# Keys and values of the second block by Strassen's product, and scores issued one head ahead

## Chip, cores and metric

The kernel runs on one core of a Trainium2 chip. The metric is the device time of one execution in microseconds; the kernel before takes 1948.06 us, the median of 3 runs (1947.14 to 1948.31).

## The reference

Two transformer-like blocks in float32 on 256 tokens of width 2048. The first (an mLSTM and a gated delta net side by side) is not touched. The second takes its output x and a context ctx of 256 tokens:

```python
hx = rmsnorm(h, norm_g) * (1.0 + scale) + shift            # 256 x 2048
hc = rmsnorm(ctx, norm_g) * (1.0 + scale_c) + shift_c      # 256 x 2048
qa, ka, va, ga, qb, kb, vb, gb = jnp.split(hx @ wi, 8, axis=-1)     # 1024 columns each
ka_c, va_c = jnp.split(hc @ wi[:, DA_WIDTH:3 * DA_WIDTH], 2, axis=-1)
kb_c, vb_c = jnp.split(hc @ wi[:, NA_OFF + NA_WIDTH:NA_OFF + 3 * NA_WIDTH], 2, axis=-1)
oa = diff_attention(qa, ka, va, ka_c, va_c, ...) * jax.nn.silu(ga)      # 8 heads, 2 softmaxes each, rope
ob = neighbourhood_attention(qb, kb, vb, kb_c, vb_c, ...) * jax.nn.silu(gb)   # 8 heads, bias
h = h + gate * (jnp.concatenate([oa, ob], axis=-1) @ w_out)
```

Only keys and values are needed for both inputs: the same weights meet hx and hc, 512 rows together. Queries and gates are needed for hx alone.

## The kernel before

Every product of activations and weights is made of three matmuls in float32r: an operand is split into hi (a copy, ACT) and lo (the rest, DVE), and hi hi, hi lo and lo hi are summed in PSUM. `split_w` (L127) splits a weight tile of 128x1024 that `load_w` fetched on SP's queue (4 raw buffers, 3 pairs of split ones); the two split instructions have a higher priority. `proj_T` (L136) has the weights stationary and 256 tokens moving and gives a transposed result (queries, keys); `proj` (L152) has tokens stationary and 512 weight columns moving (values, gates, outputs). With both inputs given, one split feeds twice the matmuls. The large PSUM tiles of both come from a pool of two (`psA`, two banks each); `side` gives single banks from a pool of four.

Block 2 (L923 on) goes through `kv`, `queries`, `gate2` and `diff_attn` for each of two groups of four heads of attention a, then through `kv` for both groups of b, and then `queries` and `near_attn` (with its gate) for each. `kv` computes keys and values and leaves them in SBUF (kT as hi and lo, V). In attention a the keys pass `rope` (L954) and their lo parts go through "nb" buffers (two of them) to the other half of the partitions by DMA on POOL's queue. The heads' work is short matmuls between instructions of DVE and ACT: two scores, maximum, exp, combination, four transposes (`pv`, L1019), product with V. `rep` (L935) is a table for attention b that is written to DRAM early on POOL's queue.

The order on each engine is made by a planner ahead of time: a list with priorities in program order, against simulated times of the instructions and the release of buffers. Later matmuls can so be put between those of a head; on the chip each engine then runs its list in order. Pools "big" tags Ah and Al hold hch and hcl (split hc), Bh and Bl hold hxh and hxl.

## Time and profile before

| | |
|---|---|
| median of 3 runs | 1948.06 us |
| the profiled execution | 1945.1 us |
| its span, first to last instruction | 1943.1 us |
| PE matmul busy | 1923.5 us, 12118 matmuls |
| DVE busy | 1336.9 us |
| ACT busy | 874.1 us |
| mean granted clock of TensorE | 0.997 |

A row of the page names line, engine, operation and tiles (out<-in), its count, and after the bar the busy time and the mean duration in ns; then the idle time of the engine before it, and what ended that. Matmul durations are modelled and overlap, so two matmuls that follow each other are priced by the distance of their starts.

### The profile page before, as it was taken

What the parts mean: (1) busy time and instruction counts of PE and PEld (TensorE: products, weight loads), DVE (VectorE), ACT (ScalarE), POOL (GpSimd) and SP (SyncE); (2) the same over time, 40 slices, a digit from 0 to 9 for tenths busy, and PEclk for the clock granted to TensorE, in tenths of its full rate; (3) what the DMA queues carried; (4) which work ended last, traced back from release to release, by engine and by line L of the source; (5) the groups of instructions that cost most, each with busy time, mean ns of one, the idle gap of its engine ahead of it and who ended that gap; (6) DMA issues with size and microseconds to landing.
All of it is one profiled execution on the core that took longest, in us unless ns stands there. A gap on an engine that the chain in (4) does not pass through costs nothing.

```text
span 1943.1 us, 30816 instructions
## 1 busy us (share of the span) xinstructions
PE 1923.5 (99%) x12118; PEld 1686.6 (87%) x12118; DVE 1336.9 (69%) x1956; ACT 874.1 (45%) x1179; POOL 240.0 (12%) x347
## 2 busy tenths in 40 slices
PE   9999999999999999999999999999999999999998
PEld 9989898999878898888888888888989989889876
DVE  6978686784648999758998856646554642269755
ACT  7645444453334443444444544634434432235553
POOL 1011010111101222002121000211111100002211
PEclk9999999999999999999999999999999999999999
DMA  9555454453546788658888767556234422279844
GB/s 293 172 167 168 142 180 151 143 178 131 168 154 211 237 262 266 204 181 298 283 281 290 252 209 240 167 137 206 94 93 157 125 76 90 96 262 329 266 148 165
DMA packets 118817, 372.70 MB, mean 192 GB/s; under 512 B 14904, under 2 KB 21480, under 8 KB 118672
## 3 DMA queue, kind: packets, MB, share of 16 engines
q1 hardware_dynamic: 95296, 314.44, 48.4%
q0 software_dynamic: 16864, 45.57, 8.4%
q10 hardware_dynamic: 6512, 10.72, 1.9%
q8 instruction: 95, 1.56, 0.3%
q14 instruction: 50, 0.41, 0.1%
HBM read 359.89 MB, written 7.64 MB: 189 GB/s over the span
## 4 chain that ended last, share of the span: by engine, by line
PE 92%; DVE 2%; DMA 2%; issue 2%; ACT 1%; POOL 0%; POOLq 0%; ACTq 0%; DVEq 0%
PE pN L163 17%; PE pN L162 17%; PE pN L164 17%; PE pT L147 10%; PE pT L149 10%; PE pT L148 10%; DMA kT<-klo 1%; DVE lo L131 1%; PE tp L1028 1%; PE p L595 1%; PE tp L1023 1%; DMA w<-in_out_dram 1%; PE pT L247 1%; ACT hi L130 0%; PE wp L642 0%
## 5 line engine op out<-in xcount | busy, mean ns | idle before, releaser
L131 DVE TENSOR_TENSOR lo<-w,hi 128x1024 fp32r<-128x1024 f32 (+1 forms) x555 | 672.9, 1215 | 423.2 <-ACT hi L130 411.5
L130 ACT ACTIVATE hi<-w 128x1024 fp32r<-128x1024 f32 (+1 forms) x555 | 580.5, 1048 | 824.7 <-PE pN L164 465.5
L163 PE MATMUL pN<-lo,uh 128*128 128x512 f32 x768 | 306.2, 399 | 0.0
L162 PE MATMUL pN<-hi,uh 128*128 128x512 f32 x768 | 305.0, 397 | 0.0
L164 PE MATMUL pN<-hi,ul 128*128 128x512 f32 x768 | 304.4, 396 | 0.0
L147 PE MATMUL pT<-uh,hi 128*128 128x256 f32 x896 | 255.5, 285 | 2.2 <-ACT kq L744 1.9
L149 PE MATMUL pT<-uh,lo 128*128 128x256 f32 x896 | 256.5, 286 | 0.0
L148 PE MATMUL pT<-ul,hi 128*128 128x256 f32 x896 | 255.7, 285 | 0.0
L162 PEld LDWEIGHTS pN<-hi,uh 128*128 128x128 f32 x768 | 144.8, 189 | 34.1
L163 PEld LDWEIGHTS pN<-lo,uh 128*128 128x128 f32 x768 | 144.8, 189 | 33.7 <-DVE lo L131 0.3
L164 PEld LDWEIGHTS pN<-hi,ul 128*128 128x128 f32 x768 | 144.8, 189 | 33.5
L147 PEld LDWEIGHTS pT<-uh,hi 128*128 128x128 f32 x896 | 168.7, 188 | 5.2 <-ACT kq L744 2.1
L149 PEld LDWEIGHTS pT<-uh,lo 128*128 128x128 f32 x896 | 168.8, 188 | 2.9 <-issue 2.4
L148 PEld LDWEIGHTS pT<-ul,hi 128*128 128x128 f32 x896 | 168.8, 188 | 1.8 <-issue 1.2
L464 DVE SCALAR_TENSOR_TENSOR ma<-m,sc,ma 128x512 f32<-128x512 f32 x240 | 169.6, 745 | 0.0
L149 PE MATMUL pT<-hxh,lo 128*128 128x256 f32 x512 | 144.8, 283 | 0.0
L147 PE MATMUL pT<-hxh,hi 128*128 128x256 f32 x512 | 144.8, 283 | 0.0
L148 PE MATMUL pT<-hxl,hi 128*128 128x256 f32 x512 | 144.6, 282 | 0.0
L162 PE MATMUL pN<-hi,hxh 128*128 128x512 f32 x256 | 101.5, 397 | 1.1 <-ACT hi L130 1.1
L163 PE MATMUL pN<-lo,hxh 128*128 128x512 f32 x256 | 101.4, 396 | 1.3 <-DVE lo L131 1.3
L454 POOL DMA_DIRECT2D m<-in_w_mod_dram x128 | 69.7, 545 | 263.2 <-DVE ma L464 208.9
L164 PE MATMUL pN<-hi,hxl 128*128 128x512 f32 x256 | 101.1, 395 | 0.0
(620 smaller groups left out, 3380.6 us busy)
## 6 DMA issues: line engine op xcount, KB each, us to landing
w<-in_dn_qkv_dram SPq DMA_DIRECT2D x88, 512.0 KB, 3.3
m<-in_w_mod_dram POOLq DMA_DIRECT2D x128, 256.0 KB, 4.1
w<-in_dn_z_dram SPq DMA_DIRECT2D x32, 512.0 KB, 3.3
w<-in_ml_v_dram SPq DMA_DIRECT2D x32, 512.0 KB, 3.6
w<-in_ml_z_dram SPq DMA_DIRECT2D x32, 512.0 KB, 4.2
w<-in_ml_o_dram SPq DMA_DIRECT2D x32, 512.0 KB, 4.1
w<-in_gate_a_dram SPq DMA_DIRECT2D x32, 512.0 KB, 4.4
w<-in_gate_b_dram SPq DMA_DIRECT2D x32, 512.0 KB, 4.4
```

Of the source, the lines that this page charges most:

```text
L130: act.activation(hi, raw, AF.Copy)
L131: ve.tensor_tensor(lo, raw, hi.bitcast(F32), ALU.subtract)
L147: pe.matmul(o, hi[:, k, :], xh[:, kt, :], start=(kt == 0), stop=False)
L148: pe.matmul(o, hi[:, k, :], xl[:, kt, :], start=False, stop=False)
L149: pe.matmul(o, lo[:, k, :], xh[:, kt, :], start=False, stop=(kt == KT - 1))
L162: pe.matmul(ps[:, t, :], xh[:, kt, s], hi[:, k, :], start=(kt == 0), stop=False)
L163: pe.matmul(ps[:, t, :], xh[:, kt, s], lo[:, k, :], start=False, stop=False)
L164: pe.matmul(ps[:, t, :], xl[:, kt, s], hi[:, k, :], start=False, stop=(kt == KT - 1))
L247: pe.matmul(o, hl[wt][:, k, :], x[:, 4 * c + k, :], start=(c == 0 and a == 0 and k == 0), stop=(c == 3 and a == 2 and k == 3))
L454: (gp if g < 8 else nc.sync).dma_start(raw, d["w_mod"][g, kt])
L464: ve.scalar_tensor_tensor(a, raw, s, a, ALU.mult, ALU.add)
L595: pe.matmul(p0, kq[:, h, 0, 0:P], kq[:, h, :, :], start=True, stop=True)
```

## The change

Each pair of key tiles, and each 512 columns of values, becomes a 2x2 block product (rows: tokens of x and of ctx; inner: halves of 2048; columns: two tiles or two halves). Seven products replace eight, in the form with 15 sums: four sums of token blocks (S1 to S4, made and split once), four of weight blocks (T1 to T4, for each pair or quarter, split after), seven of results. To make the token sums, hx and hc are kept unsplit too: hf and hcf become four tiles each, `mod_T` writes the full hx into hf, and the context part and out_b's part move to a second pool, opened after out_a. All keys and values (but group 0 of va, which stays plain and comes first) are computed before the attention and stored in DRAM (kd, vd); `kv` loads them back. The keys of a land in kraw, in the place of hch; er, eight buffers for exp, takes the same place after it. In both attentions the scores of the next head are issued before the transposes of this one; gate 0 of b comes before the heads.

The diff, cut to its core:

```diff
-        hf = hfp.tile([P, 2, 4, 512], F32, name="hf")
+        hf = [hfp.tile([P, 2, 512], F32, tag="hf", name="hf", bufs=4) for _ in range(4)]
+        tb = hfp.tile([P, 2, 4, 512], F32, tag="tb", name="tb")
...
+        sA.close()
+        hcp = sR.enter_context(tc.tile_pool(name="hcp", bufs=1, side="right", reuse_waits="tile"))
+        hcf = [hcp.tile([P, 4, T], F32, tag="hcf", name="hcf", bufs=4) for _ in range(4)]
+        s1h = hcp.tile([P, 8, T], F32R, name="s1h")
...
-            for n in range(4):
-                ct = o1.tile([P, 4, T], F32, tag="xr", name="ct")
...
-                    act.activation(hch[:, k, :], c_, AF.Identity, bias=sh)
-                    ve.scalar_tensor_tensor(hcl[:, k, :], c_, sh, hch[:, k, :].bitcast(F32), ALU.add, ALU.subtract)
...
+                act.dma_start(hcf[n], d["ctx_t"][n * 512:(n + 1) * 512, :].rearrange("(k p) t -> p k t", p=P))
...
+                    act.activation(c_, c_, AF.Identity, bias=modT[:, 2, k:k + 1])
+                act.activation(hch[:, k4, :], hcf[n], AF.Copy)
+                ve.tensor_tensor(hcl[:, k4, :], hcf[n], hch[:, k4, :].bitcast(F32), ALU.subtract)
...
+            for c in range(2):
+                s1 = hcf[2 + c]
+                ve.tensor_tensor(s1, hcf[c], s1, ALU.add)
+                act.activation(s1h[:, 4 * c:4 * c + 4, :], s1, AF.Copy)
...
+        kd = {ab: tc.dram_tile([8, P, 2, T], F32, name="kd" + ab) for ab in "ab"}
...
+        with ExitStack() as s5:
...
+            s2h, s4h = (st.tile([P, 8, T], F32R, name=nm) for nm in ("s2h", "s4h"))
...
+            def value0(i):
+                vp = proj(d["va"], 0, [(HX, HC)[i]])[0]
+                o = st.tile([P, 2, 512], F32, tag="stg", name="stg", bufs=4)
+                act.activation(o, vp, AF.Copy)
+                gp.dma_start(vd["a"][0][:, 2 * i:2 * i + 2, :], o)
...
+            value0(1)
+            value0(0)
+            v4 = lambda a: a.rearrange("p (a b) t -> p a (b t)", a=2)
+            lo1, lo2, lo4 = [], [], []
+            for c in range(2):
+                h1, h2, f1, f2 = hf[c], hf[2 + c], v4(hcf[c]), v4(hcf[2 + c])
+                ve.tensor_tensor(f1, h1, f1, ALU.subtract)
+                ve.tensor_tensor(h1, f2, h1, ALU.subtract)
+                ve.tensor_tensor(h2, h2, h1, ALU.subtract)
+            for full, hi, lo, pool in ((hcf[0:2], hch, hcl, None), (hcf[2:4], s1h, lo1, hcp),
+                                       (hf[0:2], s2h, lo2, hcp), (hf[2:4], s4h, lo4, hfp)):
+                for c in range(2):
+                    f = full[c] if full[c].shape[1] == 2 else v4(full[c])
+                    k4 = slice(4 * c, 4 * c + 4)
+                    h_ = v4(hi[:, k4, :])
+                    if hi is not s1h:
+                        act.activation(h_, f, AF.Copy)
+                    if pool is not None:
+                        tg = "hcf" if pool is hcp else "hf"
+                        lo.append(pool.tile([P, 4, T], F32R, tag=tg, name="sl", bufs=4))
+                    l_ = v4(lo[:, k4, :] if pool is None else lo[c])
+                    ve.tensor_tensor(l_, f, h_.bitcast(F32), ALU.subtract)
...
+            A11, A12, A22 = (of(hxh), of(hxl)), (of(hxh, 8), of(hxl, 8)), (of(hch, 8), of(hcl, 8))
+            S1, S2 = (of(s1h), of2(lo1)), (of(s2h), of2(lo2))
+            S3, S4 = (of(hch), of(hcl)), (of(s4h), of2(lo4))
+            TT = hfp.tile([P, 4, 1024], F32, tag="tb", name="TT")
+            ALL = slice(0, T)
...
+            def keys(ab, j):
...
+                B11, B12, B21, B22 = (raw_w(w[j + c, r], 8, P) for r in range(2) for c in range(2))
+                T1, T2, T3, T4 = (TT[:, i, :].rearrange("p (k c) -> p k c", k=8) for i in range(4))
+                ps = [psA.tile([P, 2, 2, T], F32, tag="p", name="pK").rearrange("p a b t -> p (a b) t"),
+                      side([P, 2, T], name="pK"), side([P, 2, T], name="pK")]
+                P1, P6, P5, P3, P7, P4, P2 = (p[:, i] for p, n in zip(ps, (4, 2, 1)) for i in range(n))
...
+                def prod(ps, A, B):
+                    hi, lo = split_w(B, 8, P)
+                    for k in range(8):
+                        pe.matmul(ps, hi[:, k, :], A[0](k, ALL), start=(k == 0), stop=False)
+                        pe.matmul(ps, hi[:, k, :], A[1](k, ALL), start=False, stop=False)
+                        pe.matmul(ps, lo[:, k, :], A[0](k, ALL), start=False, stop=(k == 7))
+                prod(P1, A11, B11)
+                act.activation(c1, P1, AF.Copy)
+                prod(P2, A12, B21)
+                ve.tensor_tensor(o[:, 0, 0], P2, c1, ALU.add)
+                ve.tensor_tensor(T1, B12, B11, ALU.subtract)
+                ve.tensor_tensor(T3, B22, B12, ALU.subtract)
+                ve.tensor_tensor(T2, B22, T1, ALU.subtract)
+                ve.tensor_tensor(T4, B21, T2, ALU.subtract)
+                prod(P3, S4, B22)
+                prod(P5, S1, T1)
+                prod(P6, S2, T2)
+                ve.tensor_tensor(c1, P6, c1, ALU.add)
+                ve.tensor_tensor(u4, P5, c1, ALU.add)
+                ve.tensor_tensor(o[:, 1, 0], P3, u4, ALU.add)
+                prod(P7, S3, T3)
+                ve.tensor_tensor(c1, P7, c1, ALU.add)
+                ve.tensor_tensor(o[:, 1, 1], P5, c1, ALU.add)
+                prod(P4, A22, T4)
+                ve.tensor_tensor(o[:, 0, 1], P4, c1, ALU.add)
+                for c in range(2):
+                    gp.dma_start(kd[ab][j + c], o[:, c])
...
+            def values(ab, g):
...
+                w = d["v" + ab]
+                pp = [psA.tile([P, 2, 512], F32, tag="p", name="pV") for _ in range(2)]
+                P1, P2, P3, P4 = (pp[i][:, b, :].rearrange("p (t c) -> p t c", t=2) for i in range(2) for b in range(2))
+                P5, P6, P7 = (side([P, 2, T], name="pV") for _ in range(3))
...
+                    for t in range(2):
+                        s = slice(t * P, (t + 1) * P)
+                        for k in range(2):
+                            kt = 2 * q + k
+                            pe.matmul(ps[:, t, :], A[0](kt, s), hl[0][:, k, :], start=(kt == 0 and t == 0), stop=False)
+                            pe.matmul(ps[:, t, :], A[0](kt, s), hl[1][:, k, :], start=False, stop=False)
+                            pe.matmul(ps[:, t, :], A[1](kt, s), hl[0][:, k, :], start=False, stop=(kt == 7 and t == 1))
...
+                H = (slice(0, T), slice(T, 512))
+                for q in range(4):
+                    W1, W2 = raw_w(w[g, q], 2, 512), raw_w(w[g, q + 4], 2, 512)
+                    B11, B12, B21, B22 = W1[:, :, H[0]], W1[:, :, H[1]], W2[:, :, H[0]], W2[:, :, H[1]]
+                    TQ = TT[:, 2 * (q % 2):2 * (q % 2) + 2, :].rearrange("p a (b k c) -> p a b k c", b=2, k=2)
+                    hi, lo = (wsp.tile([P, 2, T], F32R, tag=tg, name=tg) for tg in ("hi", "lo"))
+                    with tc.high_priority(offset=100):
+                        act.activation(hi, B11, AF.Copy)
+                        ve.tensor_tensor(lo, B11, hi.bitcast(F32), ALU.subtract)
+                    prod(P1, A11, (hi, lo), q)
+                    hl = split_w(W2, 2, 512)
+                    prod(P2, A12, [x[:, :, H[0]] for x in hl], q)
+                    prod(P3, S4, [x[:, :, H[1]] for x in hl], q)
+                    ve.tensor_tensor(TQ[:, 0, 0], B12, B11, ALU.subtract)
+                    ve.tensor_tensor(TQ[:, 0, 1], B22, B12, ALU.subtract)
+                    ve.tensor_tensor(TQ[:, 1, 1], B22, TQ[:, 0, 0], ALU.subtract)
+                    ve.tensor_tensor(TQ[:, 1, 0], B21, TQ[:, 1, 1], ALU.subtract)
+                    for a, pr in enumerate((((P5, S1), (P7, S3)), ((P4, A22), (P6, S2)))):
+                        hl = split_w(TQ[:, a].rearrange("p b k c -> p (b k) c"), 4, T)
+                        for b in range(2):
+                            prod(*pr[b], [x[:, 2 * b:2 * b + 2, :] for x in hl], q)
+                c1 = st.tile([P, 2, T], F32, tag="tm", name="tm", bufs=2)
+                act.activation(c1, P1, AF.Copy)
+                def put(r, c, a, b):
+                    o = st.tile([P, 2, T], F32, tag="stg", name="stg", bufs=4)
+                    ve.tensor_tensor(o, a, b, ALU.add)
+                    gp.dma_start(vd[ab][g][:, 2 * r:2 * r + 2, H[c]], o)
+                put(0, 0, P2, c1)
+                ve.tensor_tensor(c1, P6, c1, ALU.add)
+                u4 = st.tile([P, 2, T], F32, tag="tm", name="tm", bufs=2)
+                ve.tensor_tensor(u4, P5, c1, ALU.add)
+                put(0, 1, P3, u4)
+                ve.tensor_tensor(c1, P7, c1, ALU.add)
+                put(1, 1, P5, c1)
+                put(1, 0, P4, c1)
...
+            for ab in "ab":
+                for j in range(0, 8, 2):
+                    keys(ab, j)
+                for g in range(2):
+                    if (ab, g) != ("a", 0):
+                        values(ab, g)
+        sR.close()
...
         def rope(ps, scale):
-            a = a2.tile([P, 2, T], F32, tag="nb", name="ra")
-            act.activation(a, ps, AF.Copy, scale=scale)
+            a = ps
+            if scale is not None:
+                a = a2.tile([P, 2, T], F32, tag="nb", name="ra")
+                act.activation(a, ps, AF.Copy, scale=scale)
...
-                ps = proj_T(d["k" + ab], 4 * g + 2 * j, 2, [HX, HC])
...
-            vps = proj(d["v" + ab], g, [HX] if split_v else [HX, HC])
...
+            if not roped:
+                raw = kT[:, 1].bitcast(F32)
+                gp.dma_start(raw, kd[ab][4 * g:4 * g + 4].rearrange("j p c t -> p j c t"))
+                for j in range(2):
+                    hh = slice(2 * j, 2 * j + 2)
+                    act.activation(kT[:, 0, hh], raw[:, hh], AF.Copy)
+                    ve.tensor_tensor(kT[:, 1, hh], raw[:, hh], kT[:, 0, hh].bitcast(F32), ALU.subtract)
...
+                    for c in (1, 0):
+                        src = kraw[:, 4 * g + 2 * j:4 * g + 2 * j + 2, c, :]
+                        src, lo = (src, a2.tile([P, 2, T], F32, tag="nb", name="klo")) if c else rope(src, None)
+                        lo = lo.bitcast(F32R)
...
+            gp.dma_start(V, vd[ab][g])
...
+                    e = er[:, en[0] % 8, :]
+                    en[0] += 1
+                    act.activation(e, sp, AF.Exp, bias=nm, accum_out=s0[:, h, i:i + 1])
...
+            U_ = [(t, h) for t in range(2) for h in range(4)]
+            nxt = scores(*U_[0])
+            for n, (t, h) in enumerate(U_):
+                e, nxt = nxt, scores(*U_[n + 1]) if n < 7 else None
+                if h == 0:
+                    o_ = side([P, 4, P], name="o_")
+                pv(e, V, h, o_[:, h, :])
+                if n == 3:
+                    G = gate2(g, "a")
...
+            G = gate2(g, "b", O[:, 1].rearrange("p a b c -> p a (b c)")) if g == 0 else None
...
+            U_ = [(h, t) for h in range(4) for t in range(2)]
+            nxt = scores(*U_[0])
+            for n, (h, t) in enumerate(U_):
+                e, nxt = nxt, scores(*U_[n + 1]) if n < 7 else None
+                o_ = pv(e, V, h)
+                act.activation(O[:, t, h, :], o_, AF.Copy, scale=sn[:, t, h:h + 1])
...
+        kraw = big.tile([P, 8, 2, T], F32, tag="Ah", name="kraw")
+        for j in range(0, 8, 2):
+            gp.dma_start(kraw[:, j:j + 2], kd["a"][j:j + 2].rearrange("j p c t -> p j c t"))
+        two = big.tile([P, 2, 2, 4, T], F32R, tag="Al", name="two")
+        QL = [a2.tile([P, 2, 4, T], F32R, tag="O", name="qlo", bufs=1), two[:, 1]]
+        for qlo in QL:
+            for i, r in enumerate(R):
+                gp.memset(qlo[R[1 - i], i].bitcast(F32), 0.0)
+        KA = [kv(0, "a", True)]
+        QA = [queries(0, "a", True, None, QL[0])]
+        KA.append(kv(1, "a", True))
+        er, en = big.tile([P, 8, 512], F32, tag="Ah", name="er"), [0]
+        diff_attn(0, *KA[0], QA[0], QL[0])
+        QA.append(queries(1, "a", True, two[:, 0], QL[1]))
+        diff_attn(1, *KA[1], QA[1], QL[1])
```

## Rows read from the trace of the kernel before

**Rows 1.** The page, table of engines: busy us, share of the span, instructions.
```profile
PE 1923.5 (99%) x12118; PEld 1686.6 (87%) x12118; DVE 1336.9 (69%) x1956; ACT 874.1 (45%) x1179; POOL 240.0 (12%) x347
```

**Rows 2.** Stages: length, PE, PEld, DVE, ACT, POOL busy (instructions), clock, DMA.
```profile
1243.00:1870.00 627.00, 624.55 (x4024) 564.75 (x4023) 345.10 (x474) 254.59 (x365) 76.95 (x90) 1.00 0.50 159
600.00:800.00 200.00, 200.00 (x1072) 171.79 (x1071) 190.38 (x284) 88.52 (x116) 40.48 (x71) 1.00 0.77 250
1236.00:1257.00 21.00, 21.00 (x156) 19.68 (x155) 16.77 (x28) 15.82 (x26) 8.99 (x13) 1.00 0.47 151
1340.00:1470.00 130.00, 130.00 (x803) 116.06 (x802) 74.41 (x115) 53.86 (x85) 17.55 (x18) 1.00 0.37 113
1686.00:1870.00 184.00, 183.93 (x1076) 160.61 (x1075) 129.07 (x172) 84.97 (x125) 24.56 (x30) 1.00 0.75 254
```

**Rows 3.** Timeline of PE, first and last of 99 starts of 256 columns.
```profile
1261.50 0.28 PE L149 MATMUL pT<-hxh,lo 128*128 128x256 f32 x1
...
1273.13 0.28 PE L148 MATMUL pT<-hcl,hi 128*128 128x256 f32 x1
```

**Rows 4.** Timeline of PE, first and last of 47 starts of 512 columns.
```profile
1602.52 0.39 PE L162 MATMUL pN<-hi,hxh 128*128 128x512 f32 x1
...
1613.21 0.40 PE L163 MATMUL pN<-lo,hch 128*128 128x512 f32 x1
```

**Rows 5.** DVE by line and form: busy us, mean ns, idle before.
```profile
L131 DVE TENSOR_TENSOR lo<-w,hi 128x1024 fp32r<-128x1024 f32 x539 | 662.2, 1231 | 414.4 <-ACT hi L130 403.5 <-PE tp L1023 7.8 <-issue 0.3
...
L1050 DVE TENSOR_REDUCE nm<-sp 128x1 f32<-128x512 f32 x32 | 20.9, 683 | 12.0 <-PE sp L1048 11.9
...
L1057 DVE SCALAR_TENSOR_TENSOR e<-e,fl,e 128x512 f32<-128x512 f32 x16 | 12.0, 751 | 0.5
...
L1098 DVE TENSOR_TENSOR sp<-sp,nb 128x256 f32<-128x256 f32 x16 | 6.8, 428 | 8.1 <-PE sp L1097 8.1
...
L960 DVE TENSOR_TENSOR rb<-rb,cfb 128x512 f32<-128x512 f32 x8 | 7.7, 965 | 0.1
...
L1056 DVE SCALAR_TENSOR_TENSOR fl<-fl,nlam,s 128x1 f32<-128x1 f32 x16 | 6.6, 412 | 0.5
...
L959 DVE STREAM_SHUFFLE rb<-ra 128x512 f32<-128x512 f32 x8 | 5.9, 740 | 0.1
...
L987 DVE TENSOR_TENSOR klo<-pT,kT 64x512 fp32r<-64x512 f32 x8 | 5.5, 685 | 1.4 <-ACT kT L986 1.3
...
L1151 DVE TENSOR_TENSOR y<-pN,mr 128x512 f32<-128x512 f32 x6 | 3.8, 681 | 2.1 <-PE pN L164 2.1
```

**Rows 6.** ACT by line and form.
```profile
L130 ACT ACTIVATE hi<-w 128x1024 fp32r<-128x1024 f32 x539 | 570.8, 1060 | 821.0 <-PE pN L164 465.5 <-PE pT L148 250.5 <-issue 73.1
```

**Rows 7.** Chain of waits, whole run: start us, us, what.
```profile
1272.36 13.41 DMA kT<-klo
...
1367.23 0.89 PE o__13119 L1028 x8
```

**Rows 8.** DMA issues: count, KB each, median us to landing.
```profile
hd<-hf POOLq DMA_DIRECT2D x4, 512.0 KB, 5.9
...
kT<-klo POOLq DMA_DIRECT2D x8, 128.0 KB, 4.5
...
rep<-rb POOLq DMA_DIRECT2D x1, 930.0 KB, 21.9
```

**Rows 9.** Timeline of DVE at the first rope; in brackets idle before and releaser.
```profile
1271.37 0.69 DVE L987 TENSOR_TENSOR klo<-pT,kT 64x512 fp32r<-64x512 f32 x1 [0.66 <-ACT kT L986]
...
1285.90 0.01 DVE L959 LOAD_MASK_SELECT rb<-ra  x1 [10.08 <-DMA kT<-klo]
...
1303.92 0.01 DVE L959 LOAD_MASK_SELECT rb<-ra  x1 [2.92 <-DMA kT<-klo]
```

**Rows 10.** Timeline of PE at the same place.
```profile
1291.72 0.50 PE L162 MATMUL pN<-hi,hxh 128*128 128x512 f32 x1 [1.11 <-ACT hi L130]
1292.98 0.50 PE L163 MATMUL pN<-lo,hxh 128*128 128x512 f32 x1 [0.76 <-DVE lo L131]
```

187 lines of the change are left out of this document (92 added, 95 removed).

## The prediction

> **What bounds the kernel now.** I read the page's table of engines first: PE is busy 1923.5 us, 99% of the span, DVE 69% [rows 1]. A busy PE is not a full one, so the second view is the busy time by stage [rows 2]. The change lies in block 2, which runs from 1243 us on; there PE is idle for 2.45 of 627 us, DVE for 45%. The third view is the timeline of PE inside a pure stream: 98 matmuls of 256 columns start in 11.63 us, 0.1187 us each [rows 3]; 46 of 512 columns in 10.69 us, 0.2324 us each [rows 4]. The profile's 0.28 and 0.39 us for one of them overlap the next, so the distance of starts is the price. Block 2 is a queue of matmuls at that pace with next to no holes: a matmul taken away is time saved, a hole put in is time lost.
>
> **What is removed.** Keys: the change works on a pair of head tiles; before, 2 tiles x 2 halves x 8 k x 2 inputs x 3 = 192 matmuls of 256 columns, now 7 products x 8 k x 3 = 168. Eight pairs (four of ka, four of kb) save 192 x 0.1187 = 22.8 us. Values: a 512-column unit was 192 matmuls of 512 columns (44.6 us), is 7 x 4 x 12 = 336 of 256 (39.9 us). Three of four units change (va 0 stays as it was): 14.2 us. Together -37.0 us. The 2.45 us of holes [rows 2] lie where the prologue of the first keys is redone; I count -2.
>
> Here a rule speaks against the change. Two halves cost 0.2374 us where one whole costs 0.2324 [rows 3, 4], so cutting a matmul costs 5 ns, and that is in the sum. The Trainium skill ("TensorE: Matmul & The Clock Gate", Back-to-back issue gap) gives a sustained 131 ns at 512 columns and 81 ns at 128; an estimate from that page for 256, 98 ns, would make the values 23 us dearer and the keys 19 us cheaper, a loss of some 4 us before any wait. This trace disagrees with both figures.
>
> **What is added on DVE and ACT, and what hides it.** A pair of keys needs 7 splits in place of 4: 7 lo subtractions of 1.231 us, 4 weight sums of the same 128x1024 size (as the same row), 7 additions out of PSUM of 0.428 us: 16.5 us of DVE beside 168 x 0.1187 = 19.9 us of PE; ACT 7 x 1.060 = 7.4 us [rows 5, 6]. A value unit: per quarter one half split (0.685), three whole ones (1.231), four sums of 128x512 (0.685), at the end 7 additions of 0.685: 33.3 us of DVE beside 39.9. So DVE stands at 83% in this stage. Cover: from 600 to 800 us DVE is busy 190.4 of 200 us and PE 200 [rows 2]. I take the work itself as hidden.
>
> Waits in the stage, two kinds. (a) The products P7 and P4 of a pair lie in one PSUM bank. No row of before shows a matmul that waits for a read of the other half of its bank; if P4 waits for the addition that reads P7, a pair loses the end of a matmul (0.28 us [rows 3]) and 0.43 of DVE: between 0 and 8 x 0.71 = 5.7 us. I take 2, nearer to nothing, as matmuls of the next pair, in other banks, can stand in between. The Trainium skill ("PSUM — Partial Sum Buffer", PSUM bank collisions raise a hardware error) has PE's write and DVE's read of one bank kept apart by the program; by that rule alone the term is 5.7. (b) Value units hold both large PSUM tiles: P3 of the next unit waits for five or six additions of 0.69 us, 4.1 us, less the 2.85 us of its P1 and P2; three changes of unit, 0 to 1.5 us each: 3.
>
> **The start.** The token sums (S1 to S4) need the finished hx. Between 1236 and 1257, where hx is made, DVE is busy 16.8 of 21 us [rows 2]. Six sums and eight lo subtractions, 14 x 1.23 = 17 us, come after or into that; also the splits of va 0 (one per 2.8 us of PE now, where a key split fed 5.7 us) and the first pair's. From 1236 to P3's start at about 1272 (22.3 us of va 0 from 1243, P1 and P2 5.7, transposes 1) DVE has 36 us, and is asked for the 16.8 of that row, five more splits (6.2), three of the pair (3.7) and 17: 44; P5 behind it needs the weight sums, 4.9 + 1.2 more in 2.85 us. Bounds 0 (all fits idle time) and 8 + 3 = 11; I take 6.
>
> The plain parts of block 1 that move (the ctx statistics to after out_a, four copies of hch, the S1 sums) lie beside 89 us of out_b matmuls; ACT adds 6 x 1.06 us. If that cover failed, the stage would lose these 6 us. New DMAs on POOL's queue: 16 stores of keys and 12 of values of 256 KB, 2 of va 0; 4 + 2 + 4 loads back. Each store lies tens of us ahead of its load.
>
> **Attention a, where the cover goes.** Before, heads of diff_attn ran between K/V matmuls, DVE 74.4 of 130 us [rows 2]. Now queries and gates alone are left. A head costs DVE 2 x 0.683 + 0.751 + 0.412 = 2.53 us (a reciprocal left out), PE 4 x 0.2324 + 8 x 0.111 = 1.82 us [rows 5, 7]. Over the part: PE 45.5 (queries) + 44.6 (gates) + 16 x 1.82 = 119 us; DVE 32 splits (39.4), key and query rope and splits (eight ropes of 0.740 + 0.965 + 0.685, 24 half splits of 0.685: 35.6), heads 40.5, gates 2.4: 118 us. DVE comes level with PE, so what DVE loses is no longer given back.
>
> Two losses. First, the rope of the keys: kraw takes the place of hch, so its loads start when the last product ends (some 5.9 us, as for hd [rows 8]). Then eight pieces pass two "nb" buffers, each freed when its kT DMA lands (4.5 us). Before, DVE stood 10.08 us for such a landing [rows 9], which took 13.41 us [rows 7]; the DMA had been queued on POOL's queue behind rep (930 KB, 21.9 us). PE's holes from it were 1.11 and 0.76 us [rows 10], since three splits held 17 us of key matmuls. Three splits of queries hold 3 x 2.85 = 8.5 us, and "rep" is still ahead of these DMAs: 13.4 - 8.5 = 5 us. What is queued behind the wait on DVE are the query splits, and PE behind them. Second, er takes kraw's place, so no exp runs before the keys of both groups are done: 5.9 + four times 8.3 us (a rope's 2.4, two half splits, a landing) + rep's 21.9 = 61 us at most. PE has queries 0, gate 0, queries 1 until then, 68 us, if the planner puts them ahead; then eight heads run uncovered, 8 x (2.53 - 1.82) = 6 us. If only queries 0 stands ahead, PE waits 61 - 22.8 = 38 us. Bounds 0 and 38; I take 5 + 6 and 2 for the shorter landings (2.92 us of DVE's wait at the next, not all of it PE's) = 13, nearer to what the holes in rows 10 show.
>
> **Attention b and the end.** K/V of b were already done before near_attn; in 1686 to 1870 PE is full, DVE 129 of 184 [rows 2]. Scores one head ahead help the uncovered last heads: -1 (0 to -3).
>
> **Sum**, against the profiled execution (span 1943.1, its time 1945.1 us; the median of the runs is 3.0 above): -37 - 2 + 5 + 6 + 13 - 1 = -16, so 1929 there, 1932 as a median.
>
> **Rivals.** (1) All waits are filled: -37 - 2 - 3 + 4 = -38, 1910. For it: 627 us with 2.45 idle, by the same planner. Against: DVE level with PE in attention a. (2) DVE becomes the bound of the product stage: its additions wait for the end of a product, with splits queued behind. At 0.66 us for each of seven (as DVE waits for ACT in [rows 9]), a pair is 21.1 us of DVE to 19.9 of PE: 8 x 1.2 = 10 us more, 1942. Against: DVE at 95% with a full PE. (3) Slower: PE stands in front of the first heads until the keys of both groups are roped, because matmuls later in its queue can't pass a waiting one. Price up to 38 us; from 29 us there on (with 6 + 5 - 1 elsewhere) the gain of 39 is gone; at 38 it is +9, 1957. For it: the 13.4 us landing that DVE waited for in full. Against: 68 us of other matmuls are at hand. (4) A matmul's fixed part eats the saving: the products are 240 matmuls more and 86,016 columns less (38.2 us at 0.444 ns a column, from the two streams). At 5 ns each the 240 cost 1.2 us; at 159 ns nothing is saved, and with the waits above (24) it is 1972. Against: two streams of this very form at 5 ns [rows 3, 4]. The Trainium skill's figures above would be an estimated 65 ns.
>
> **Chances.** Forecast (1921 to 1943) 0.50, (1) 0.22, (2) 0.10, (3) 0.16, (4) 0.02. About 0.2%, 4 us, is what a measurement of this kernel tells from no change. Faster: 0.47 + 0.22 + 0.05 = 0.74; same: 0.03 + 0.05 + 0.02 = 0.10; slower 0.16. The range runs from (1) to the middle of (3): 1910 to 1953.
>
> **What would show it.** PE's matmuls go from 12118 to 12118 + 240 (2304 of K/V become 2544), DVE's busy time up by about 183 us (8 x 11.6 + 3 x 23.4 + 20). Pairs of keys should start every 20 us, value units every 40. Start: a hole before P3 and P5 of the first pair. Attention a: an idle PE between the end of the products and the first exp, DVE waiting for kT. I am wrong if the products run slower than 0.12 us a matmul, if DVE's share of the stage exceeds 95%, or if the hole in front of the first heads is over 25 us.

## The result, and the profile after

The changed kernel takes **1969.8 us** (median; 1967.8 to 1971.9), the kernel before 1948.2 in the same session: a ratio of **1.0112, 95% interval [1.0095, 1.0130]**. It is 21.6 us slower where 16 us faster was forecast, and outside the range. The profiled execution took 1970.46 us, its span 1968.7, 25.6 us more than before's 1943.1.

The page of the changed kernel, busy us of each engine, its share and its instructions (the answer to [rows 1]):
```profile
PE 1904.7 (97%) x12358; PEld 1683.4 (86%) x12358; DVE 1500.9 (76%) x2161; ACT 926.7 (47%) x1236; POOL 264.4 (13%) x389
```
PE has the 240 matmuls more that were forecast and is busy 18.8 us less, and yet the span is longer. So PE stands idle or runs at a lower clock somewhere. The windows say where (start:end, length, then busy us of PE, its weight loads, DVE, ACT and POOL, granted clock, DMA share, GB/s):
```profile
1130.00:1200.00 70.00, 64.27 (x265) 51.34 (x264) 50.69 (x61) 44.76 (x77) 1.84 (x3) 0.95 0.74 248
1240.00:1280.00 40.00, 36.90 (x164) 29.85 (x164) 37.33 (x48) 28.46 (x40) 6.64 (x9) 0.91 0.47 155
1280.00:1577.00 297.00, 296.83 (x2493) 295.65 (x2492) 230.84 (x273) 119.78 (x128) 22.98 (x36) 1.00 0.42 145
1577.00:1640.00 63.00, 41.86 (x222) 35.77 (x222) 30.62 (x39) 22.39 (x28) 17.69 (x24) 0.84 0.67 178
1640.00:1760.00 120.00, 110.92 (x688) 97.72 (x687) 97.16 (x151) 66.69 (x110) 26.80 (x33) 0.97 0.54 165
1760.00:1850.00 90.00, 88.72 (x561) 78.95 (x560) 80.61 (x130) 50.01 (x84) 19.32 (x24) 1.00 0.79 267
1850.00:1900.00 50.00, 44.39 (x233) 35.10 (x232) 43.18 (x68) 25.33 (x49) 8.39 (x10) 0.97 0.90 305
```
These are out_b, the start of block 2, the product stage, the beginning of attention a, its heads, its end with attention b, and attention b's last heads with the beginning of the output product. Where [rows 2] had 2.45 us idle in 627, the beginning of attention a alone has 21 in 63, and at 0.84 of the clock. For the loss with the clock in it I use one measure throughout, **lost time**: for each matmul the distance to the next start, less the median distance of its width in the same trace, summed over a stretch. Only distances above the median count; the shorter ones, some 10 us in each of the three kernels, are left out. The stretches are fixed times, and a faster kernel is further on in its work at the same time, so sums to the end are safer to compare than single rows.

| lost time, us | before | changed | repaired (below) |
|---|---|---|---|
| 1000 to 1130 (out_a) | 1.3 | 1.0 | 6.3 |
| 1130 to 1200 (out_b) | 0.6 | 9.8 | 2.5 |
| 1240 to 1280 (start) | 1.2 | 6.9 | 5.7 |
| 1280 to 1577 (product stage) | | 3.1 | 4.9 |
| 1577 to 1640 | | 26.1 | 8.9 |
| 1640 to 1760 | | 15.6 | 9.6 |
| 1760 to the end | 7.0 | 18.6 | 10.3 |
| 1200 to the end | 18.5 | 70.6 | 39.7 |

(In the kernel before, products and attentions share the stretch from 1280 to 1760, with 9.9 us lost in all.) From 1130 on the change loses 61.3 us more; the matmuls themselves (the medians, summed from there to the end) need 757.8 us for 794.4, 36.6 less. That makes 24.7 us, where the spans differ by 25.6.

**The product stage is as forecast.** In 1280 to 1577 PE is full and DVE at 78%; the waits of that window list none for PE. The starts keep the pace of [rows 3], 0.12 us:
```profile
1319.74 0.28 PE L1013 MATMUL pK<-hxh,lo 128*128 128x256 f32 x1
1319.86 0.28 PE L1011 MATMUL pK<-hxh,hi 128*128 128x256 f32 x1
1319.98 0.28 PE L1012 MATMUL pK<-hxl,hi 128*128 128x256 f32 x1
1320.10 0.28 PE L1013 MATMUL pK<-hxh,lo 128*128 128x256 f32 x1
```
The Trainium skill's figures for the gap between matmuls ("TensorE: Matmul & The Clock Gate", Back-to-back issue gap), by which the products would have gained nothing, are not what this trace shows. P7 and P4 of a pair never met in their bank: in all eight pairs 1.5 us or more of other matmuls stand between them, as the forecast argued, and DVE's read of P7 is over before P4 begins (in the second pair 1319.82 and 1322.00). So the Trainium skill's rule that the program keeps PE's writes and DVE's reads of one bank apart ("PSUM — Partial Sum Buffer", PSUM bank collisions raise a hardware error) cost no wait here.

**The beginning of attention a.** PE's timeline (start us, us of one, what; in brackets the idle time before and what ended it):
```profile
1605.59 0.40 PE L164 MATMUL pN<-hi,hxl 128*128 128x512 f32 x1
1605.82 0.40 PE L162 MATMUL pN<-hi,hxh 128*128 128x512 f32 x1
1621.91 0.80 PE L163 MATMUL pN<-lo,hxh 128*128 128x512 f32 x1 [15.69 <-DVE lo L131]
1622.50 0.63 PE L164 MATMUL pN<-hi,hxl 128*128 128x512 f32 x1
1622.93 0.63 PE L162 MATMUL pN<-hi,hxh 128*128 128x512 f32 x1
```
A product of the first gate stands 15.69 us for a split, and afterwards matmuls start 0.43 us apart instead of 0.23: the granted clock is at the lower of its two levels (1.2 of 2.4 GHz) after the hole. Why the split was late, DVE's timeline:
```profile
1600.44 1.41 DVE L1163 TENSOR_TENSOR klo<-kraw,kT 64x512 fp32r<-64x512 f32 x2 [5.33 <-DMA kT<-klo]
1601.88 1.23 DVE L131 TENSOR_TENSOR lo<-w,hi 128x1024 fp32r<-128x1024 f32 x1
1620.01 0.01 DVE L1134 LOAD_MASK_SELECT rb<-kraw  x1 [16.90 <-DMA kT<-rb]
1620.65 1.21 DVE L131 TENSOR_TENSOR lo<-w,hi 128x1024 fp32r<-128x1024 f32 x1
```
The split (L131) was queued behind the next key rope (L1134), which waited 16.90 us for a kT piece to free its nb buffer, where [rows 9] had 10.08. POOL's timeline shows what stood ahead of that piece:
```profile
1583.21 1.06 POOL L1166 DMA_DIRECT2D V<-vda  x2
1584.27 0.64 POOL L1165 DMA_DIRECT2D kT<-klo  x1
1586.14 0.66 POOL L1165 DMA_DIRECT2D kT<-klo  x1
1586.79 0.85 POOL L1108 DMA_DIRECT2D rep<-rb  x1
1590.42 1.31 POOL L1165 DMA_DIRECT2D kT<-rb  x2 [2.77 <-DVE rb L1163]
```
The chain of waits has that piece as its longest link there (start, us), and the DMA issues of 1580 to 1640 give the times to landing:
```profile
1591.14 28.73 DMA kT<-rb
```
```profile
V<-vda POOLq DMA_DIRECT2D x2, 1024.0 KB, 10.6
rep<-rb POOLq DMA_DIRECT2D x1, 930.0 KB, 30.7
kT<-klo POOLq DMA_DIRECT2D x4, 128.0 KB, 16.5
```
A piece of 128 KB took 28.7 us, against 13.41 in [rows 7] and 4.5 in [rows 8]; rep took 30.7 for 21.9. The two V loads ahead of it are the change's own.

**Out_b.** DVE there:
```profile
1155.78 5.22 DVE L888 SCALAR_TENSOR_TENSOR hcf<-hcf,gx,rsb 128x256 f32<-128x256 f32 x13
1160.93 0.68 DVE L898 TENSOR_TENSOR hf<-xr,fw 128x512 f32<-128x512 f32 x1
1161.53 1.21 DVE L131 TENSOR_TENSOR lo<-w,hi 128x1024 fp32r<-128x1024 f32 x1
1172.33 1.22 DVE L883 SCALAR_TENSOR_TENSOR xr<-hf,xr 128x1024 f32<-128x1024 f32 x1 [3.25 <-DMA xr<-in_x_dram]
```
Thirteen modulations of ctx stand in a row ahead of a split, later an x tile comes late; PE waits 2.64 us for the first split, 3.09 us at the second place, and the window's clock is 0.95.

**The end.** The modulation's ring mr (60 steps of 0.744 us on DVE) shows its first and last start, first in the kernel before, then in the changed one:
```profile
L464 DVE SCALAR_TENSOR_TENSOR mr<-mr,sc x60: 731/747/1785, 1718.6 to 1820.4; 128x512 f32<-128x512 f32 x60
```
```profile
L464 DVE SCALAR_TENSOR_TENSOR mr<-mr,sc x60: 724/744/2509, 1782.8 to 1895.4; 128x512 f32<-128x512 f32 x60
```
Its memory is the place in which the change keeps the second group's queries (two), so it starts 186 us before the end of the span instead of 224, and is done 73 us before it instead of 123, beside the last heads.

### The profile page after: what moved, and what is told of

It reads as the page before. It is cut to its first block, busy times and chain, and to the rows that moved or that the text cites. A ratio compares the mean times of both kernels' runs of the same rounds, so it can differ in the third digit from the quotient of the medians.

```text
span 1968.7 us, 31698 instructions
## 1 busy us (share of the span) xinstructions
PE 1904.7 (97%) x12358; PEld 1683.4 (86%) x12358; DVE 1500.9 (76%) x2161; ACT 926.7 (47%) x1236; POOL 264.4 (13%) x389
## 4 chain that ended last, share of the span: by engine, by line
PE 79%; DMA 7%; DVE 6%; issue 4%; ACT 2%; POOL 1%; ACTq 0%; DVEq 0%; POOLq 0%; SPq 0%
PE pN L164 13%; PE pN L163 13%; PE pN L162 13%; PE pT L147 6%; PE pT L149 6%; PE pT L148 6%; PE pK L1013 3%; PE pK L1011 3%; PE pK L1012 3%; DMA mr<-in_w_mod_dram 2%; PE pV L1049 2%; PE pV L1051 2%; PE pV L1050 2%; DVE lo L131 2%; DMA kT<-rb 2%
## 5 line engine op out<-in xcount | busy, mean ns | idle before, releaser
L130 ACT ACTIVATE hi<-w 128x1024 fp32r<-128x1024 f32 (+1 forms) x535 | 558.7, 1047 | 730.3 <-PE pN L164 407.1
L131 DVE TENSOR_TENSOR lo<-w,hi 128x1024 fp32r<-128x1024 f32 (+1 forms) x535 | 648.0, 1214 | 265.3 <-ACT hi L130 260.3
L130 ACT ACTIVATE hi<-TT 128x1024 fp32r<-128x1024 f32 x56 | 59.6, 1065 | 77.8 <-PE pK L1012 55.7
L163 PE MATMUL pN<-lo,hxh 128*128 128x512 f32 x160 | 66.3, 414 | 21.7 <-DVE lo L131 21.7
L131 DVE TENSOR_TENSOR lo<-TT,hi 128x1024 fp32r<-128x1024 f32 x56 | 68.4, 1222 | 21.0 <-ACT hi L130 20.7
L147 PE MATMUL pT<-hxh,hi 128*128 128x256 f32 x256 | 73.4, 287 | 2.4 <-DVE G L1192 2.4
L149 PE MATMUL pT<-hxh,lo 128*128 128x256 f32 x256 | 73.0, 285 | 2.0 <-DVE lo L131 2.0
L148 PE MATMUL pT<-hxl,hi 128*128 128x256 f32 x256 | 72.9, 285 | 0.0
```

What stands on the lines that cost most here:

```text
L130: act.activation(hi, raw, AF.Copy)
L131: ve.tensor_tensor(lo, raw, hi.bitcast(F32), ALU.subtract)
L147: pe.matmul(o, hi[:, k, :], xh[:, kt, :], start=(kt == 0), stop=False)
L148: pe.matmul(o, hi[:, k, :], xl[:, kt, :], start=False, stop=False)
L149: pe.matmul(o, lo[:, k, :], xh[:, kt, :], start=False, stop=(kt == KT - 1))
L163: pe.matmul(ps[:, t, :], xh[:, kt, s], lo[:, k, :], start=False, stop=False)
```

## The experiments

Times are medians; "before" was run beside each and lay between 1946.1 and 1948.7.

**Is it rep?** Moved to the beginning of the product stage:
```
             value0(1); value0(0)
+            rep = ...; rb = st.tile([8, 465], F32, tag="stg", ...); (the same two DMAs)
-        rep = ...; rb = a2.tile(...); gp.dma_start(rb, d["rpb"]); gp.dma_start(rep, rb x 64)   # attention a
```


> The changed kernel (1969.8 us) with the load of the position biases and the write of rep (930 KB on POOL's queue) moved from in front of the kT pieces of attention a to the beginning of the product stage; nothing else moves and nothing is left out. Theory (rep's transfer stands ahead of the kT pieces, DVE waits 16.9 us for one of them, the query and gate splits queue behind it and PE falls to half clock): the 15.85 us hole of PE at the gate product and most of the half-clock stretch after it go, 1946 us (1940 to 1953). Rival A (the rope chain itself, with its two nb buffers, is what DVE waits for): a hole of 8 us or more stays there, 1960 to 1966. Rival B (DVE is level with PE through attention a): other holes of the same sum take its place, 1964 to 1970.


Measured 1964.0 us (1960.8 to 1965.4). The hole of 15.69 us is gone (lost time in 1577 to 1640: 8.7 for 26.1), but the product stage loses 12.7 us more and 1760 to 1900 another 6.4. In the product stage DVE shows
```profile
1303.63 1.23 DVE L1023 TENSOR_TENSOR TT<-w 128x1024 f32<-128x1024 f32 x1 [11.85 <-DMA w<-in_ka_dram]
```
a weight load delayed beside rep. The trace is the theory's, the time a rival's: the hole was rep's, and rep took much of its price along.

Moved into block 1 (same two DMAs, ahead of the mLSTM stage), in the changed kernel and in the kernel before:


> The changed kernel (1969.8 us) with the load of the position biases and the write of rep moved into block 1, to the beginning of the mLSTM stage, far from the kT pieces and from the product stage's weights; nothing else is moved or left out. With rep at the beginning of the product stage 1964.0 us was measured: the holes of attention a's first 80 us fell from 33.4 to 12.3 us, and a hole of 9.4 us came in the product stage, where DVE waited for a weight load that ran beside rep's 22 us. Theory (rep's transfer is in the way wherever other loads are due, and costs about 21 us ahead of the kT pieces): 1949 us (1944 to 1955). Rival A (it collides with the mLSTM stage's weight loads just as it did with the product stage's): 1958 to 1966. Rival B (attention a's loss is the rope chain and only shifted): 1962 to 1970.

> The kernel before (1948.2 us) with rep written at the beginning of the mLSTM stage; nothing else is moved or left out. In the kernel before DVE waited 10.08 us for a kT piece behind rep as well, but PE had the K and V products of the same stage to do. Theory (rep costs only where such cover is gone): 1945 to 1949. Rival (rep cost the kernel before the same, and the change's loss is something else): 1925 to 1940.


Measured 1963.0 us and, in the kernel before, 1952.9 (ratio 1.0027 [1.0017, 1.0038]). Rival A for the first: 600 to 800 loses 14.9 us for 5.3, where three weight loads took 18.8 us in the median instead of 3.2 (DMA issues of 595 to 640):
```profile
w<-in_ml_v_dram SPq DMA_DIRECT2D x3, 512.0 KB, 18.8
rep<-rb POOLq DMA_DIRECT2D x1, 930.0 KB, 22.7
```
In the kernel before the same move costs 4.3 us, more than either of its expectations: rep stood better where it was, beside K and V matmuls.

Left out altogether (attention b reads its position biases from another DRAM tile instead, so that the reads stay):
```
-        rep = ...; (rb, its load, the write of rep)
+        rep = hd
```


> The changed kernel (1969.8 us) without rep: its load and its 930 KB write are left out, and the position biases of attention b are read from another DRAM tile of finite numbers (same number and size of reads), so that the whole price of this one transfer shows. Theory (rep costs the changed kernel about 20 us, at the gate product of attention a, and nothing takes its place): 1949 us (1944 to 1954). Rival (what stands there is the rope chain, and the wait only moves): 1959 to 1968.

> The kernel before (1948.2 us) without rep, in the same way (position biases read from another DRAM tile; rep's load and write left out). Theory (in the kernel before PE had K and V products to do beside it, so the transfer cost 3 to 6 us, about what the excess of its first 60 us shows): 1944 us (1941 to 1947). Rival (it cost the kernel before as much as the changed one): 1924 to 1935.


Measured 1958.4 us (1952.7 to 1960.9) and 1944.1: rep costs the changed kernel 11.4 us and the kernel before 3.3. The second is the theory's number; the first lies just under the rival's. But the hole is gone: in 1577 to 1640 DVE waits 2.0 us for kT pieces (19.6 in the changed kernel), with the V loads and the order of the ropes as they were, and 8.7 us are lost for 26.1. No kT piece takes longer than 8.4 us to land, for 28.7, so the V loads ahead of it don't make that landing by themselves. The profiled run, its lowest (1952.7), shows 4.6 us of that lost again in 1760 to 1900.

In eight pieces:
```
+                    rb = st.tile([1, 465], F32, tag="stg", name="rb", bufs=4)      # after keys(ab, j)
+                    gp.dma_start(rb, d["rpb"][h:h + 1]); gp.dma_start(rep[h:h + 1], rb x 64)
```


> The changed kernel with rep written in eight pieces of 116 KB, one behind each pair of key blocks of the product stage (each through a buffer of the stage's output ring, which spaces them); nothing is left out. As one transfer at the stage's beginning it took 22 us and cost 12.7 us there (DVE waited 11.85 us for a weight load). Theory (a weight load can spare the time of a 116 KB piece, so the pieces cost nothing): as without rep, 1950 us (1946 to 1956). Rival (the bytes cost the same in pieces): 1960 to 1966.


Measured 1956.7 us, just above the theory's range, nine runs from 1946.9 to 1962.4. As cheap as without rep: a piece lands in 6.0 us, the product stage loses the same 3 us. The spread is new; the profiled run, its highest, loses 28.1 us in 1760 to 1900 (15.6 in the changed kernel), where the ring mr runs:
```profile
L464 DVE SCALAR_TENSOR_TENSOR mr<-mr,sc x60: 724/744/2621, 1769.7 to 1894.7; 128x512 f32<-128x512 f32 x60
```
It starts 13 us sooner than in the changed kernel and is done at the same time. All four kernels that are rid of the hole with mr as late as this (rep in the product stage, in block 1, left out, in pieces) lose more than the changed kernel from 1760 on: 20.6 to 29.0 us for 18.6.

**What covers the heads.** The scores in each head's own turn:
```
-            nxt = scores(*U_[0])
-                e, nxt = nxt, scores(*U_[n + 1]) if n < 7 else None
+                e = scores(t, h)
```


> The changed kernel with the scores of each head issued in the head's own turn in both attentions, as in the kernel before; all else stays, nothing is left out. Theory (attention a has no K and V products left beside it, so the lookahead is what covers the maximum, the exponential and the joining of the two maps, some 3 us a head, wherever the queries and the gate of the next group do not): 1985 us (1976 to 2000). Rival (the planner fills the waits with those products anyhow and the lookahead is worth nothing): 1967 to 1973. Second rival (the lookahead itself holds back the splits and costs time): 1955 to 1966.


Measured 2005.7 us, 36 more, above the theory's range: without K and V matmuls beside them, the heads live on the lookahead, those of attention a above all. Attention b's first scores start at 1823.4 for 1792.4, so 31 of the 36 us are lost before them.

Without the second pair of query tiles:
```
-        two = big.tile([P, 2, 2, 4, T], F32R, tag="Al", name="two")
-        QL = [a2.tile([P, 2, 4, T], ...), two[:, 1]]
+        QL = [a2.tile([P, 2, 4, T], ...)] * 2
-        QA.append(queries(1, "a", True, two[:, 0], QL[1]))
+        QA.append(queries(1, "a", True, None, QL[1]))
```


> The changed kernel without the second pair of query tiles (two): the queries of attention a's second group go into the first group's tiles, after its last head, as in the kernel before; the place of two then stands free for the modulation's ring mr from the end of the product stage. Nothing is left out. Theory (mr's 60 steps of DVE, 45 us, start at 1782.8 us instead of 1718.6 in the kernel before because two holds their place, and crowd the last heads and the output product: 11.5 us of PE's idle and half-clock time in 1850 to 1900 against 2.6 in the kernel before's same part): these fall by some 8 us, and the second group's queries come later by some 3: 1965 us (1959 to 1969). Rival (the second group's queries are what covers the first group's last heads): 1972 to 1985.


Measured 1988.7 us: the rival, for the whole. Its windows show both sides (the heads, the output product):
```profile
1640.00:1760.00 120.00, 90.81 (x536) 78.62 (x535) 107.75 (x172) 53.31 (x89) 29.70 (x36) 0.82 0.73 225
1850.00:1900.00 50.00, 50.00 (x276) 42.64 (x275) 28.30 (x42) 29.60 (x53) 7.90 (x11) 1.00 0.51 163
```
The heads lose PE 29 of 120 us and the clock, while the end, with mr done early, is full: 1.3 us lost for 11.5, as the theory had it.

Both at once: two in the place of kraw, the joined maps in four tiles in the free half of the output tiles, so that Al is free for mr after the first group:
```
-        er, en = big.tile([P, 8, 512], F32, tag="Ah", name="er"), [0]
+        ers = [at.tile([P, 2, 512], F32, tag="ma%d%d" % (1, i), name="er") for i in range(2)]
-        two = big.tile([P, 2, 2, 4, T], F32R, tag="Al", name="two")
+        two = big.tile([P, 2, 2, 4, T], F32R, tag="Ah", name="two")
+        dm = big.tile([P, 1], F32, tag="Al", name="dm"); act.activation(dm, <group 0's output>, AF.Copy)
```


> The changed kernel with the second pair of query tiles kept, but in the place of kraw, the joined maps in a ring of four (instead of eight) in the not yet used half of the attention's output tiles, so that the modulation's ring mr can start at the end of the first group's heads, some 60 us earlier. Nothing is left out. Without two, 1850 to 1900 lost 1.3 us instead of 11.5, but the second group's queries no longer covered the first group's heads (33 us). Theory (mr's late start is what crowds the end, and it can start earlier at no price): 1961 us (1955 to 1966). Rival (its 45 us of DVE work crowd attention a's second group instead, or four maps are too few): 1969 to 1980.


Measured 1963.9 us, in the theory's range: 1850 to 1900 loses 4.9 us for 11.5 and the heads no more than in the changed kernel (13.7 for 15.6), but 1800 to 1850 loses 9.5 for 2.4.

**Out_b.** The statistics of ctx ahead of out_a; six of DVE's operations on POOL; ctx through a ring; and statistics and modulation both beside out_a, straight into hch and hcl:
```
+ e4: cs, cr, spread(...) moved ahead of the out_a loop
+ e9: gp.tensor_tensor(hcl[...], hcf[n], hch[...], subtract); gp.tensor_tensor(s1, hcf[c], s1, add)
+ c2: ct = o1.tile([P, 4, T], tag="xr"); hcf[n] = ct * gx * rsb
+ d1: before out_a: ct (tag "m") -> hch, hcl;  after it: hcf[n] = hch + hcl
```


> The changed kernel with the statistics of ctx (its eight loads, their squares, the reduction and the spread) put back ahead of the first out_a product, where the kernel before had them; the modulation of ctx into hcf can then start earlier. Nothing is left out. Theory (that work, started only after out_a, crowds ahead of the weight splits of out_b on DVE and costs holes of 2.80 and 3.26 us and the half clock behind each, 9.5 us in all): 1960.5 us (1958 to 1964). Rival (DVE is short of time there in any order, or the load of xr is what is late): the holes move and 1967 to 1970 stays.

> The changed kernel with the four subtractions that make hcl and the two token sums of ctx's rows (1.22 us each on DVE) in block 1 on POOL instead of DVE; order and all else as they were, nothing left out. Theory (DVE is crowded beside out_b by the ctx part, 5.2 us of modulation in a row and these six): the second hole (3.26 us at 1172, half clock behind it) goes, the first (2.80 at 1160, behind the row of modulations) stays: 1964 us (1961 to 1967). Rival (what is late there is the load of xr, issued once out_a is done): 1968 to 1971.

> The changed kernel with ctx loaded through the two-buffer ring of the x tiles of out_b, as in the kernel before, instead of straight into the four hcf tiles; the ring lets one part of ctx at a time through, so that DVE takes four modulations at a time and not thirteen in a row. Nothing is left out. Theory (the row of modulations, not the sum of DVE's work, makes the two holes at out_b, 9.2 us with the half clock behind them): 1962 us (1959 to 1966). Rival (DVE has too much to do there in any order, as on POOL, where the time rose): 1968 to 1974.

> The changed kernel (1969.8 us) with ctx's statistics and modulation put back beside out_a, straight into hch and hcl through a ring of small tiles, as in the kernel before; the full values that the token sums need are made again later as hch + hcl (four additions on DVE beside out_a and out_b). Nothing is left out. So far: the statistics alone moved early took the loss at out_b from 9.8 to 2.8 us, but 7 us came at out_a, where DVE waited 3.65 and 2.71 us for the loads of hcf; six operations on POOL or a ring beside out_b made it no better. Theory (the change gave up the place in which this work was free, because the full-width ctx has no memory before out_a is done): 1961 us (1957 to 1965). Rival (DVE has too much to do in out_a and out_b together, wherever it stands): 1967 to 1972.


Measured 1968.3, 1975.9, 1974.4 and 1969.5 us: the theory's number never, the rival's for the first and the last, and above the rival's range too for POOL (5 us) and the ring. Early statistics clear out_b (2.8 us lost for 9.8) but PE stands 5.33 us at out_a, where DVE waits for ctx; on POOL out_b loses 11.9, and spread by the ring the holes are three (3.19, 1.33 and 1.61 us) that lose 10.0 up to 1240, as much as in the changed kernel (10.1): the row of thirteen is gone, but DVE now waits 3.44 and 4.72 us for ctx's loads, with splits queued behind. Straight beside out_a, out_a and out_b together lose 8.1 us for 10.8. My theory that only the place matters is not borne out by these; the kernel before lost 1.9 there with the same modulation, and what its order had is not settled.

**Together**: rep in pieces, ctx beside out_a, mr early; and the same without the ctx part:


> The changed kernel with three edits together: rep in eight pieces behind the key blocks (1956.7 us alone, -13), ctx's part beside out_a, and mr's early start. Nothing is left out. Theory (three separate losses, each given back): 1940 us (1933 to 1948), below both kernels. Rival (the waits of attention a take each other's place): 1950 to 1960.

> The repaired kernel (rep in pieces, ctx beside out_a, mr's early start: 1936.2 us) with ctx's part left as in the changed kernel, after out_a. Nothing is left out. Theory (ctx's part costs the changed kernel 10.8 us in 1000 to 1200 and the repaired one 8.8, so its edit is worth 2 to 3 us): 1939 us (1936 to 1943). Rival (the three need each other, as alone they gave 13, 0 and 6 us and together 34): 1946 to 1955.


Measured **1936.2 us** (1932.3 to 1937.0; ratio to before 0.9942 [0.9929, 0.9954]) and 1946.6 (0.9995 [0.9985, 1.0004]). The first, in the theory's range, beats both kernels; the second is the rival's. The page of the first and the windows that answer to the changed kernel's:
```profile
PE 1895.5 (98%) x12358; PEld 1679.7 (87%) x12358; DVE 1499.1 (77%) x2177; ACT 921.4 (48%) x1233; POOL 275.1 (14%) x403
```
```profile
1130.00:1200.00 70.00, 68.30 (x295) 55.17 (x294) 42.84 (x38) 30.14 (x40) 1.13 (x2) 1.00 0.71 236
1577.00:1640.00 63.00, 57.12 (x356) 51.62 (x355) 50.29 (x68) 32.59 (x44) 20.28 (x27) 0.95 0.77 220
1640.00:1760.00 120.00, 115.74 (x739) 103.62 (x738) 109.72 (x184) 69.83 (x120) 27.53 (x29) 0.99 0.75 229
1850.00:1900.00 50.00, 49.25 (x242) 39.69 (x242) 32.00 (x40) 27.90 (x47) 8.42 (x5) 1.00 0.48 159
```
The matmuls are the same, and from 1577 to 1640 PE loses 8.9 us where the changed kernel lost 26.1. Pieces gave 13 us alone, mr 6, both 23: what fits is that with rep out of the way the end waits for mr, and with mr early it waits less. It still waits: in the second kernel mr's steps run until 1834.9, and DVE and PE show in attention b
```profile
1823.82 0.75 DVE L464 SCALAR_TENSOR_TENSOR mr<-mr,sc 128x512 f32<-128x512 f32 x1 [0.74 <-DMA mr<-in_w_mod_dram]
1825.17 0.75 DVE L464 SCALAR_TENSOR_TENSOR mr<-mr,sc 128x512 f32<-128x512 f32 x1 [0.60 <-DMA mr<-in_w_mod_dram]
1826.64 1.44 DVE L464 SCALAR_TENSOR_TENSOR mr<-mr,sc 128x512 f32<-128x512 f32 x1 [0.72 <-DMA mr<-in_w_mod_dram]
1828.01 0.42 DVE L1298 TENSOR_TENSOR sp<-sp,nb 128x256 f32<-128x256 f32 x1
```
```profile
1831.62 1.11 PE L1201 MATMUL tp<-ident,e 128*128 128x128 f32 x4 [6.09 <-ACT e L1302]
```
Three steps of mr, each waiting for its own load, stand on DVE ahead of one head's addition (L1298); the head's exponential comes late, and PE stands 6.09 us. This is how the ring crowds the heads. In the first kernel the longest wait of PE for an exponential there is 1.3 us.

The ctx part gives 0.3 us alone and 10.4 on top of the other two, and it saves less than 2 us at out_a and out_b. The rest shows as that one hole and as 3 us less lost in the first 600, where nothing was changed and where the traces of the changed kernels lie between 43 and 47 us. Why the hole is in the one kernel and not in the other stays open.

**The products by themselves.** Plain products in the changed and in the repaired kernel:
```
-            prod(P1, A11, B11) ... prod(P4, A22, T4)          # and the sums S1 to S4
+            ps = proj_T(d["k" + ab], j, 2, [HX, HC])          # values: proj(d["v" + ab], g, [HX, HC])
```


> The changed kernel with plain products in the product stage (x and ctx each times the whole weight, as the kernel before), their results copied to the same DRAM tiles; the 15 sums and their splits are left out, the rest stays (lookahead, place of the stage, rep). Theory (PE sets the end of the product stage, and the stage runs without a gap in both forms): the stage is longer by the 37 us of the forecast, the start shorter by up to 6 us that the sums hold up, so 2002 us (1994 to 2009). Rival (Strassen's form gives back part of its gain to the unit changes, the banks or DVE): 1975 to 1990.

> The repaired kernel (1936.2 us) with plain products in the product stage; the token sums and their splits are left out. In the changed kernel plain products took 26.3 us more, not the forecast's 37, while the PE time that the products need rose by the full amount and the waits of attention a came out smaller. Theory (Strassen's form is worth its 37 us where the waits behind it are the same, plus nothing for the start that it holds up by 5): 1968 us (1964 to 1974), 32 more. Rival (it is worth 26 in any frame): 1959 to 1963.


Measured 1996.2 us (+26.3) and 1974.4 (+38.2). In the first PE is busy 1942.5 us, 37.8 more, but loses 13 us less from 1200 on than the changed kernel; in the frame without those waits the full price shows, more than either of its expectations gave: over the whole span the matmuls' medians rise by 35.6 us and the lost time by 1.2.

## Why the prediction was wrong

- **Products, -37.0**: right. PE needs 36.6 us less between the two traces, and 38.2 is what plain products cost in the repaired kernel.
- **Product stage, +5**: too much; the waits for banks and at the change of units don't show, 3.1 us are lost in all. For the banks the forecast's own argument held, matmuls of the next pair in between. DVE is busy 164 us more over the span, where 183 were forecast, and 78% of the stage, where 83% were.
- **Start, +6**: the size right, 5.7 more than before, and the cause, DVE crowded by the token sums; the place wrong. No hole of a microsecond stands before P3 or P5. It is earlier, in va 0: PE waits 3.10 us for an hxl that DVE makes behind a sum, the subtraction for one and a split, and nearly 3 more go to the half clock behind it, which the forecast had not counted. In both plain kernels the stretch loses 0.9. That the sizes agree is in part luck.
- **Attention a, +13 with -2 and the stage's +5 beside it, 16 in all**: the step that failed first, and the largest; 34.9 us more were lost (44.8 from 1280 to 1760, for 9.9). "Three splits of queries hold 8.5 us, and rep is still ahead: 13.4 - 8.5 = 5" took the landing of before for that of after. The piece took 28.7 us: two V loads of 1 MB now stand on the same queue ahead of it and the weights of queries and gate run beside it, and rep itself took 30.7 (how the 28.7 divide was not tried; without rep, with the same V loads, no piece took over 8.4 and DVE's wait is 2.0). The half clock behind the hole was not in the sum at all. That splits queue on DVE behind the rope was forecast, and the price was wrong. Rival (3) came nearest, with PE standing ahead of the first heads; its cause, that the keys of both groups must be roped before the first exponential, is not what held PE: without rep the hole is gone with that order unchanged. Rep explains 11.4 us of the kernel's time and 17 of this stretch; the rest of the 34.9 lies in the heads, where queries, gates and lookahead cover less than K and V did (8 us were forecast, 15.6 are lost).
- **The moved parts of block 1, nothing, "if that cover failed 6"**: failed; 9.2 us. The cover was counted as PE's 89 us; what held PE was a split late on DVE, behind thirteen operations in a row and behind a late x tile. That an order without this price exists is not shown: none of the four edits brought the stretch back to what the kernel before loses there.
- **Attention b and the end, -1**: failed; 11.6 us more. I priced the scores and did not follow the memory: the place given to two is where mr had stood, and the 45 us of DVE that were done beside K and V came 38 us later against the end. The kernel without two and the one with two moved lose 12.2 and 16.6 us from 1760 on for 18.6, so this is a part of it; the rest of the 11.6 is not settled.
- **The lookahead** was priced through the heads' 6 us; taking it away costs 36.

The terms that failed sum to 34.9 - 16 + 9.2 + 12.6 = 41 us; the forecast of -16 and the 25.6 of the spans are 41.6 apart.

None of the three signs of being wrong that the prediction named came: the products ran at 0.12 us a matmul, DVE stood at 78% in their stage, and the longest hole ahead of the first heads was 15.69 us and not over 25. The loss is made of several holes, each below that mark. The measured time lies next to the 1972 of rival (4), but by chance: its cause, a dearer matmul, is what the pace of 0.12 us excludes. Nor does the repaired kernel's 1936.2, inside the forecast's range, bear the forecast out, as its three edits were no part of it.

## What to carry to other kernels

Work that is saved on the busiest engine was also the cover of other waits: list each wait beside it, with the durations that the changed queue will have, before the saving is booked. When a tile moves to new memory, ask what stood there and when that can now start. A kernel with several such losses may give little back until all are mended: here 13 and 6 us alone, 34 us together.
